# Gate projections drained by ScalarE and multiplied by the norm later, query transposes moved behind the value products

## The chip, the core and the metric

The kernel runs on one core of one Trainium2 chip. The core's engines run side by side, each through its own list of instructions in order: TensorE (PE, with its weight loads as PEld) multiplies matrices into PSUM, VectorE (DVE) and ScalarE (ACT) work elementwise on PSUM and SBUF, GpSimd (POOL) on SBUF, and SyncE (SP) issues DMAs. Semaphores order work across engines. The metric is device time in microseconds (us) of one execution.

## The reference

One layer of a hybrid decoder, batch 1, 512 tokens, width 1024, in fp32:

```python
h = rmsnorm(x, g_mix)
x_rnn, g_rnn, q, k, v, gate_a, gate_b = split(h @ w_in)
y_a = (rg_lru(causal_conv(x_rnn)) * gelu(g_rnn)) @ w_rnn_proj
y_b = window_attention(rope(rmsnorm(q)), rope(rmsnorm(k)), v, sinks) @ w_attn_proj
merged = sigmoid(gate_a) * y_a + sigmoid(gate_b) * y_b
x = x + merged @ w_out
x = x + square(relu(rmsnorm(x, g_mlp) @ w_up)) @ w_down
x = x + (p @ w_ple_proj) * sigmoid(rmsnorm(x, g_ple) @ w_ple_gate)
```

There are 16 query heads and 4 key-value heads of width 64; the window is 128 tokens, worked in four blocks of 128.

## The kernel before

All large products are made of three fp32r matmuls each, on weights and activations that are split into a high and a low part. A unit of weights (128 x 1024) comes from HBM, ACT writes its high part `wh` (line 118) and DVE the low part `wl` (line 119); `wload` keeps about three units ahead. The order on PE, ACT, SP and POOL is the order of the code (`manual_schedule`). DVE is not in that list: its order is set by the framework's scheduler, which may put an instruction far from where it stands in the code.

The change lies in the attention loop, eight turns `u` (four blocks of tokens for each half of the heads). The norm of x is not applied to the activations; `rb` holds the reciprocal norm of every token, and results are multiplied by it. Each turn has two groups of four heads, `g` = 0 and 1, and two gate projections, `p0` and `p1`, of 24 matmuls each, which fill PE between the steps of the softmax. On PE a turn is:

scores `S` of group 0; projection `p0`; transposes `ppt` of the previous turn's group 1 probabilities; scores of group 1; the previous turn's products with the values, `po`; the first half of `p1`; the transposes `pqt` of the next turn's queries; the second half of `p1`; transposes `ppt` of this turn's group 0.

For each group the softmax runs over the engines: ACT (or DVE, in the first block) copies scores out of PSUM into `sm`, DVE masks, takes the maximum and four small steps on `st` (lines 457 to 468), ACT takes the exponentials with their sums (474, 477), DVE adds and inverts (482, 483), POOL scales the probabilities in four instructions (486), PE transposes them and DVE masks the result into `pt`, twice (505), which `po` reads. `sm` has two buffers, the score bank `S` one.

The queries are turned by `q_rope` on DVE (lines 405 to 408: `ra`, twice `rb`, and `ra` again), transposed on PE, and split into `qt` by ACT (423) and DVE (425). A gate projection is taken out of PSUM by DVE, which multiplies it by `rb` (596); its sigmoid comes later, in the recurrent branch (750) or ahead of the merge (798).

Of the kernel before, what the change touches and what calls it, by code (L numbers as in the profile page):

```python
# [9 lines left out]
F32 = mybir.dt.float32  # L10
F32R = mybir.dt.float32r
AF = mybir.ActivationFunctionType
ALU = mybir.AluOpType
# [57 lines left out]
def layer_kernel(ctx, tc, w_all, x_t, p_t, vecs, row, ctab, out_t):  # L71
    nc = tc.nc
# [19 lines left out]
    def ftile(name):  # L92
        return act.tile([P, S], F32, tag="f", name=name, bufs=F_BUFS)
# [11 lines left out]
    def wissue(parts=1):  # L105
        u = order.pop(0)
        ready[u] = wsplit(u, wp, W_BUFS, parts)
# [15 lines left out]
    def wload(u):  # L123

        while u not in ready or (order and len(ready) <= AHEAD):
            wissue()
        return ready.pop(u)
# [110 lines left out]
    def s_ps(name):  # L238
        return ps.tile([P, 4, 256], F32, tag="S", name=name, bufs=1)

    def s_banks(name):
        wide = s_ps(name).rearrange("p a b -> p (a b)")
        return [wide[:, 0:S], wide[:, S : 2 * S]]
# [151 lines left out]
    def q_rope(u):  # L395
        n = u % NB
        src = q_raw.pop(u).rearrange("p (h d) -> p h d", d=HD)
        a = ftile(f"ra_{u}").rearrange("p (h d) -> p h d", d=HD)
        b = ftile(f"rb_{u}").rearrange("p (h d) -> p h d", d=HD)
        tt = nc.vector.tensor_tensor  # L400

        def tb(t, lo, hi):
            return t[:, n, lo:hi].unsqueeze(1).broadcast_to([P, 8, hi - lo])

        tt(out=a, in0=src, in1=tb(ccq, 0, HD), op=ALU.mult)
        tt(out=b[:, :, 0:32], in0=src[:, :, 32:64], in1=tb(ssq, 0, 32), op=ALU.mult)
        tt(out=b[:, :, 32:64], in0=src[:, :, 0:32], in1=tb(ssq, 32, 64), op=ALU.mult)
        tt(out=a, in0=a, in1=b, op=ALU.add)
        q_rot[u] = a

    def q_transpose(u, pt=None):


        a = q_rot.pop(u)
        pt = tr_ps(f"pqt{u}") if pt is None else pt
        for i in range(4):
            nc.tensor.transpose(pt[:, i * P : (i + 1) * P],
                                a[:, 2 * i : 2 * i + 2, :].rearrange("p a d -> p (a d)"), ident)
        qt = [att.tile([P, 4, P], F32R, tag="qt", name=f"qt{u}{j}", bufs=4) for j in range(2)]
        rows = [slice(0, HD), slice(HD, P)]  # L420
        src = [pt[own].rearrange("p (i t) -> p i t", t=P) for own in rows]
        for j, own in enumerate(rows):
            nc.scalar.activation(qt[j][own], src[j], AF.Copy)
        for j, own in enumerate(rows):
            nc.vector.tensor_tensor(out=qt[j][rows[1 - j]], in0=src[j],
                                    in1=qt[j][own].bitcast(F32), op=ALU.subtract)
        q_t[u] = qt

    def window(u):
        n = u % NB  # L430
        return max(n - 1, 0), (2 if n else 1)
# [78 lines left out]
    def pv(u):  # L510
        po = mm_ps(f"po{u}")
        b0, nb = window(u)
        for kb in range(nb):
            for g in range(2):
                kv = 2 * (u // NB) + g
                nc.tensor.matmul(po[g * HD : (g + 1) * HD, :],
                                 vt[:, b0 + kb, kv * HD : (kv + 1) * HD],
                                 p_t_.pop((u, g, kb)), start=kb == 0, stop=kb == nb - 1)
        return po.rearrange("p (i t) -> p i t", t=P)

    def o_split(u, po):
        t = slice(u % NB * P, (u % NB + 1) * P)
        oj = o[u // NB]
        nc.scalar.activation(oj[:, :, 0, t], po, AF.Copy)
        nc.vector.tensor_tensor(out=oj[:, :, 1, t], in0=po, in1=oj[:, :, 0, t].bitcast(F32),
                                op=ALU.subtract)
# [49 lines left out]
    def q_first():  # L576
# [5 lines left out]
    qkv_group(2, q_banks, [  # L582
        lambda: (k_transpose(norm["rot"]), q_first()),
        k_double,
        lambda: q_transpose(0, s_banks("pqt0")[0]),
    ])
    rb = norm["x"]
    q_evac(1, q_banks)
# [4 lines left out]

    def gate_evac(pg, name):
        gt = ftile(name)
        nc.vector.tensor_tensor(out=gt, in0=pg, in1=rb, op=ALU.mult)
        gates.append(gt)

    fills = [U_GB + m for m in range(KC)] + [U_GA + m for m in range(KC)]

    for u in range(8):
        w0 = wload(fills[len(gates)])
        p0 = mm_ps(f"pgate_{u}_0")
        s0 = scores(u, 0)
        softmax_max(u, 0, s0)
        proj(p0, w0, xg)
        if u:
            p_transpose(u - 1, 1)
            p_evac(u - 1, 1)
        softmax_exp(u, 0)  # L610
        if u < 7:
            q_rope(u + 1)
        softmax_norm(u, 0)
        if u < 6:
            q_scale(u + 2)
        gate_evac(p0, f"gate_{u}_0")
        s1 = scores(u, 1)
        if u:
            o_split(u - 1, pv(u - 1))
        softmax_max(u, 1, s1)  # L620
        w1 = ready.pop(fills[len(gates)])
        p1 = mm_ps(f"pgate_{u}_1")
        proj(p1, w1, xg, range(0, CUT))
        if u < 7:
            q_transpose(u + 1)
        wissue()
        softmax_exp(u, 1)
        softmax_norm(u, 1)
        proj(p1, w1, xg, range(CUT, KC))
        gate_evac(p1, f"gate_{u}_1")  # L630
        p_transpose(u, 0)
        p_evac(u, 0)
# [91 lines left out]
    for m in range(KC + LAG):  # L724
        if m < KC:
            w = wload(U_X + m)
            px = mm_ps(f"px{m}")
            proj(px, w, xg, range(0, 5))
            if m == 0:
                p_transpose(7, 1)  # L730
                p_evac(7, 1)
            proj(px, w, xg, range(5, 8))
            if m == 0:
                po = pv(7)
                o_split(7, po)
                att_scope.close()
                rnn = rnn_scope.enter_context(tc.tile_pool(name="rnn", bufs=1))
                gw += wsplit(U_GATE, rnn, 1)
        if py_last:
            att_evac(*py_last)  # L740
        for f in later.pop(0):
            f()
        later.append([])
        if m < KC:
            x_scale(m, px)
        units = gate_units((m - 3, m - 2)) if m in (3, 5, 7) else []
        if m < KC:
            x_conv(m)
        for gt in gb[m : m + 1]:
            nc.scalar.activation(gt, gt, AF.Sigmoid)  # L750
        if m >= LAG:
            w = wload(U_ATT + m - LAG)
            py_last = m - LAG, mm_ps(f"pyb{m - LAG}")
            for g in units:
                gate_post(*g)
            proj(py_last[1], w, o)
        if len(batch) == 2:
            take_pair()
# [6 lines left out]
    for m in range(KC):  # L765
# [4 lines left out]
        pg = mm_ps(f"pgl{m}")  # L770
# [24 lines left out]

    mg = rtiles("mg")
    for gt in ga:
        nc.scalar.activation(gt, gt, AF.Sigmoid)
    first = [(wload(U_RNN + m), mm_ps(f"pya{m}")) for m in range(2)]
    for w, py in first:  # L800
# [16 lines left out]
    for m in range(KC):  # L817
# [3 lines left out]
        po = mm_ps(f"pout{m}")  # L821
# [65 lines left out]
    for m in range(KC):  # L887
        w = wload(U_PG + m)
        pg = mm_ps(f"ppg{m}")
# [90 lines left out]
```

## Time and profile before

| | us |
|---|---|
| median of 3 runs | 838.13 (837.47, 838.13 and one of 2166.76) |
| the profiled execution | 837.6 |
| its span, first to last instruction | 835.5 |
| PE busy | 829.4 |
| DVE busy | 522.1 |
| ACT busy | 365.0 |
| POOL busy | 101.4 |
| granted TensorE clock, mean | 0.999 |

Busy time is the sum of an engine's recorded instructions. PE's records overlap each other, since matmuls are pipelined, and a matmul that starts late behind a wait can be recorded as part of a longer busy stretch; so PE's share says that little else ends the kernel, and the spacing of its starts says how long each thing takes. The profiled execution is 0.5 us under the median and 2.1 us longer than its span.

### The profile page before, as it was taken

The numbers are of one execution on the slowest core, as the hardware profiler recorded it, in microseconds if no ns is written. First come the engines' busy times: TensorE is split into PE (matmuls) and PEld (weight loads), VectorE is DVE, ScalarE is ACT, GpSimd is POOL, SyncE is SP. The second block draws the span as 40 slices with busy tenths as digits, with TensorE's granted clock in tenths as the row PEclk, the third lists the DMA queues.
The fourth block names the chain that finished last, engine by engine and source line by source line (L and its number), as shares of the span: only waits on it lengthen the run. The fifth ranks groups of instructions, "written<-read, shape, count | busy, mean of one in ns | idle before, by whom it ended". The sixth has DMA issues, their size and how long they took to land.

```text
span 835.5 us, 9915 instructions
## 1 busy us (share of the span) xinstructions
PE 829.4 (99%) x3780; PEld 678.9 (81%) x3780; DVE 522.1 (62%) x768; ACT 365.0 (44%) x581; POOL 101.4 (12%) x123
## 2 busy tenths in 40 slices
PE   9999999999999999999999999999999999999997
PEld 7888877877888888888888888888888888888886
DVE  4687798886766878486567533653355435655563
ACT  7434665663578895633343221231222212333430
POOL 2922432421011110000210000000000000012100
PEclk9999999999999999999999999999999999999999
DMA  7344122122232232235333322223223232233141
GB/s 251 126 115 138 51 80 72 51 77 76 76 100 76 76 102 100 76 127 186 131 103 109 104 98 102 89 89 119 86 97 100 101 102 76 100 102 101 51 163 39
DMA packets 25744, 84.00 MB, mean 101 GB/s; under 512 B 3040, under 2 KB 3424, under 8 KB 25696
## 3 DMA queue, kind: packets, MB, share of 16 engines
q1 hardware_dynamic: 25552, 83.32, 30.0%
q8 instruction: 30, 0.49, 0.2%
q14 instruction: 18, 0.15, 0.1%
q10 hardware_dynamic: 144, 0.05, 0.0%
HBM read 80.20 MB, written 2.10 MB: 99 GB/s over the span
## 4 chain that ended last, share of the span: by engine, by line
PE 99%; DMA 0%; DVE 0%; ACT 0%; issue 0%
PE pu L145 7%; PE pd L145 7%; PE pd L147 7%; PE pu L147 7%; PE pd L146 7%; PE pu L146 7%; PE pq L258 5%; PE pgate L145 4%; PE pgate L147 4%; PE pgate L146 4%; PE pkv L258 3%; PE pyb L145 2%; PE S L441 2%; PE px L145 2%; PE pgl L145 2%; PE pyb L146 2%
## 5 line engine op out<-in xcount | busy, mean ns | idle before, releaser
L119 DVE TENSOR_TENSOR wl<-wr,wh 128x1024 fp32r<-128x1024 f32 (+1 forms) x144 | 180.6, 1257 | 56.1 <-ACT wh L118 56.1
L118 ACT ACTIVATE wh<-wr 128x1024 fp32r<-128x1024 f32 (+1 forms) x144 | 149.7, 1045 | 130.5 <-PE pd L146 98.5
L146 PE MATMUL pu<-x1g,wh 128*128 128x512 f32 x256 | 99.6, 389 | 0.0
L145 PE MATMUL pu<-x1g,wh 128*128 128x512 f32 x256 | 99.6, 389 | 0.0
L147 PE MATMUL pu<-x1g,wl 128*128 128x512 f32 x256 | 99.6, 389 | 0.0
L145 PE MATMUL pd<-u,wh 128*128 128x512 f32 x256 | 99.6, 389 | 0.0
L146 PE MATMUL pd<-u,wh 128*128 128x512 f32 x256 | 99.6, 389 | 0.0
L147 PE MATMUL pd<-u,wl 128*128 128x512 f32 x256 | 99.6, 389 | 0.0
L131 ACT ACTIVATE u<-up 128x512 fp32r<-128x512 f32 x32 | 20.2, 633 | 124.4 <-DVE up L847 124.4
L213 POOL TENSOR_TENSOR sq<-sq,sq_x 128x512 f32<-128x512 f32 x14 | 18.2, 1298 | 453.5 <-ACT sq_x L211 453.5
L856 DVE TENSOR_TENSOR xr<-pd,xr 128x512 f32<-128x512 f32 x32 | 22.1, 692 | 81.5 <-PE pd L147 81.5
L147 PEld LDWEIGHTS pu<-x1g,wl 128*128 128x128 f32 x256 | 48.0, 188 | 10.1
L147 PEld LDWEIGHTS pd<-u,wl 128*128 128x128 f32 x256 | 48.0, 188 | 10.0
L146 PEld LDWEIGHTS pd<-u,wh 128*128 128x128 f32 x256 | 48.0, 188 | 10.0
L146 PEld LDWEIGHTS pu<-x1g,wh 128*128 128x128 f32 x256 | 48.1, 188 | 10.0
L145 PEld LDWEIGHTS pd<-u,wh 128*128 128x128 f32 x256 | 48.0, 188 | 9.9
L145 PEld LDWEIGHTS pu<-x1g,wh 128*128 128x128 f32 x256 | 48.0, 188 | 9.9
L145 PE MATMUL pgate<-xg,wh 128*128 128x512 f32 x128 | 51.4, 402 | 0.0
L147 PE MATMUL pgate<-xg,wl 128*128 128x512 f32 x128 | 50.2, 392 | 0.0
L146 PE MATMUL pgate<-xg,wh 128*128 128x512 f32 x128 | 50.0, 391 | 0.0
L846 DVE TENSOR_TENSOR up<-pu,rb_x 128x512 f32<-128x512 f32 x32 | 22.0, 691 | 40.2 <-PE pu L147 40.1
L474 ACT ACTIVATE sm<-sm,st,sc 128x128 f32<-128x128 f32 x64 | 30.8, 483 | 23.6 <-DVE st L468 21.6
(225 smaller groups left out, 1620.1 us busy)
## 6 DMA issues: line engine op xcount, KB each, us to landing
wr<-in_w_all SPq DMA_DIRECT2D x142, 512.0 KB, 3.3
x<-in_x_t SPq DMA_DIRECT2D x8, 256.0 KB, 5.6
xr<-in_x_t SPq DMA_DIRECT2D x8, 256.0 KB, 3.6
out<-pgt SPq DMA_DIRECT2D x7, 256.0 KB, 2.1
kt<-kt SPq DMA_DIRECT2D x8, 128.0 KB, 2.2
wr<-in_w_all SPq DMA_DIRECT2D x2, 256.0 KB, 3.6
pk<-in_p_t SPq DMA_DIRECT2D x2, 256.0 KB, 3.8
tab<-in_ctab SPq DMA_DIRECT2D x1, 384.0 KB, 6.8
```

The costliest lines, as they stand in the source:

```text
L118: nc.scalar.activation(wh[:, c], raw[:, c], AF.Copy)
L119: nc.vector.tensor_tensor(out=wl[:, c], in0=raw[:, c], in1=wh[:, c].bitcast(F32), op=ALU.subtract)
L131: nc.scalar.activation(r[:, 0, :], src, AF.Copy)
L145: nc.tensor.matmul(out, ah, bh, start=start, stop=False)
L146: nc.tensor.matmul(out, ah, bl, start=False, stop=False)
L147: nc.tensor.matmul(out, al, bh, start=False, stop=stop)
L213: nc.gpsimd.tensor_tensor(out=acc, in0=acc, in1=t, op=ALU.add)
L258: nc.tensor.matmul(banks[n], a[:, part, n * P : (n + 1) * P], w[:, c], start=k == 0 and i == 0, stop=k == KC - 1 and i == 2)
L441: nc.tensor.matmul(pss[:, i, :], q_t[u][i % 2][:, 2 * g + i // 2, :], kt[part][:, kv, b0 * P : b0 * P + 256], start=part == 0, stop=part == 1)
L474: nc.scalar.activation(sm[:, i, :], sm[:, i, :], AF.Exp, bias=st[:, 1, i : i + 1], scale=q_sc[u][:, 4 * g + i : 4 * g + i + 1], accum_out= ...
L846: nc.vector.tensor_tensor(out=y, in0=pu, in1=r1, op=ALU.mult)
L856: nc.vector.tensor_tensor(out=x1[m], in0=pd, in1=x1[m], op=ALU.add)
```

## The change

Three edits. The gate projection leaves PSUM through ACT, as a plain copy; the product with `rb` is written in the code ahead of each gate's sigmoid. The transposes of the next queries move on PE from the middle of `p1` to the place behind `po`, in turns 1 to 6; their evacuation to `qt` stays where it was on ACT. So that the queries are turned in time, `q_rope(u + 1)` moves in the code from behind the exponentials of group 0 to the start of turn `u`.

```diff
     def q_transpose(u, pt=None):
...
-        for j, own in enumerate(rows):
-            nc.scalar.activation(qt[j][own], src[j], AF.Copy)
-        for j, own in enumerate(rows):
-            nc.vector.tensor_tensor(out=qt[j][rows[1 - j]], in0=src[j],
-                                    in1=qt[j][own].bitcast(F32), op=ALU.subtract)
         q_t[u] = qt
+        def evac():
+            for j, own in enumerate(rows):
+                nc.scalar.activation(qt[j][own], src[j], AF.Copy)
+            for j, own in enumerate(rows):
+                nc.vector.tensor_tensor(out=qt[j][rows[1 - j]], in0=src[j],
+                                        in1=qt[j][own].bitcast(F32), op=ALU.subtract)
+        return evac
...
     def gate_evac(pg, name):
         gt = ftile(name)
-        nc.vector.tensor_tensor(out=gt, in0=pg, in1=rb, op=ALU.mult)
+        nc.scalar.activation(gt, pg, AF.Copy)
...
     for u in range(8):
+        if 0 < u < 7:
+            q_rope(u + 1)
...
         softmax_exp(u, 0)
-        if u < 7:
-            q_rope(u + 1)
+        if u == 0:
+            q_rope(1)
         softmax_norm(u, 0)
...
         if u:
-            o_split(u - 1, pv(u - 1))
+            po = pv(u - 1)
+            qt_evac = q_transpose(u + 1) if u < 7 else None
+            o_split(u - 1, po)
...
         if u < 7:
-            q_transpose(u + 1)
+            (qt_evac if u else q_transpose(1))()
...
         for gt in gb[m : m + 1]:
+            nc.vector.tensor_tensor(out=gt, in0=gt, in1=rb, op=ALU.mult)
             nc.scalar.activation(gt, gt, AF.Sigmoid)
...
     for gt in ga:
+        nc.vector.tensor_tensor(out=gt, in0=gt, in1=rb, op=ALU.mult)
         nc.scalar.activation(gt, gt, AF.Sigmoid)
```

In the changed kernel the lines behind the first edit are three higher (408 stays, 425 becomes 428, 482 becomes 485), and the products with `rb` are lines 757 and 806.

First place: DVE around the exponentials of group 0 in turn 2. `st_1047` (before) and `st_1053` (after) hold the small columns of that group; L468, or L471 now, is the last step ahead of the exponentials, L482, or L485 now, the first that needs them. Before:

```order
L468 TENSOR_TENSOR st_1047<-rowb,st_1047 128x4
L505 TENSOR_TENSOR pt_1082<-ppt_1077,tab 128x512
L505 TENSOR_TENSOR pt_1084<-ppt_1077,tab 128x512
L405 TENSOR_TENSOR ra_1091<-q_518,cc_q 128x512
L406 TENSOR_TENSOR rb_1092<-q_518,ss_q 128x8x32
L407 TENSOR_TENSOR rb_1092<-q_518,ss_q 128x8x32
L482 TENSOR_TENSOR st_1047<-st_1047 128x4
L388 TENSOR_REDUCE sc_1105<-asq_1103 128x8
L408 TENSOR_TENSOR ra_1091<-ra_1091,rb_1092 128x512
L483 RECIPROCAL st_1047<-st_1047 128x4
L390 TENSOR_SCALAR sc_1105<-sc_1105,e_180 128x8
L596 TENSOR_TENSOR gate_0_1109<-pgate_0_1034,rb_x 128x512
```

The same place after:

```order
L471 TENSOR_TENSOR st_1053<-rowb,st_1053 128x4
L485 TENSOR_TENSOR st_1053<-st_1053 128x4
L486 RECIPROCAL st_1053<-st_1053 128x4
L388 TENSOR_REDUCE sc_1105<-asq_1103 128x8
L757 TENSOR_TENSOR gate_0_1109<-gate_0_1109,rb_x 128x512
L390 TENSOR_SCALAR sc_1105<-sc_1105,e_180 128x8
L528 TENSOR_TENSOR o_706<-po_1120,o_706 128x4x128
```

The two `pt` and the rope no longer stand between the step ahead of the exponentials and the step behind them; the gate's product stays in the loop.

Second place: DVE from the inversion of turn 1, group 1 (`st_958` before, `st_965` after), which releases POOL's scaling, to the small steps of turn 2, group 0. Before:

```order
L505 TENSOR_TENSOR pt_1026<-ppt_1019,tab 128x512
L482 TENSOR_TENSOR st_958<-st_958 128x4
L483 RECIPROCAL st_958<-st_958 128x4
L119 TENSOR_TENSOR wl_1030<-wr_1028,wh_1029 128x1024
L457 COPY_PREDICATED sm_1044<-tab,S_1035 128x512
L464 TENSOR_REDUCE st_1047<-sm_1044 128x4
```

After:

```order
L486 RECIPROCAL st_965<-st_965 128x4
L405 TENSOR_TENSOR ra_1028<-q_518,cc_q 128x512
L406 TENSOR_TENSOR rb_1029<-q_518,ss_q 128x8x32
L407 TENSOR_TENSOR rb_1029<-q_518,ss_q 128x8x32
L119 TENSOR_TENSOR wl_1036<-wr_1034,wh_1035 128x1024
L408 TENSOR_TENSOR ra_1028<-ra_1028,rb_1029 128x512
L460 COPY_PREDICATED sm_1050<-tab,S_1041 128x512
L508 TENSOR_TENSOR pt_1088<-ppt_1083,tab 128x512
L467 TENSOR_REDUCE st_1053<-sm_1050 128x4
L508 TENSOR_TENSOR pt_1090<-ppt_1083,tab 128x512
L468 TENSOR_TENSOR st_1053<-st_1053,sc_775 128x4
L757 TENSOR_TENSOR gate_1_1017<-gate_1_1017,rb_x 128x512
```

The rope, both `pt` of turn 1's group 1 and the product of its second gate now stand ahead of L471 of turn 2; `pt_1088` reads `ppt_1083`, PE's transposes of what POOL scales behind L486.

Third place: ACT from the exponentials of turn 1's group 1 to those of turn 2's group 0, after the change.

```order
L480 ACTIVATE st_965<-st_965 128x4
L599 ACTIVATE gate_1_1017<-pgate_1_971 128x512
L118 ACTIVATE wh_1035<-wr_1034 128x1024
L459 ACTIVATE sm_1050<-S_1041 128x512
L477 ACTIVATE sm_1050,st_1053<-sm_1050,st_1053,sc_775 128x128 x4
```

Only the gate's copy, L599, is new there; the rest stood in that order before.

## Rows read from the trace of the kernel before

**Rows 1.** The page's part 4: the chain that ended last, by engine.
```profile
PE 99%; DMA 0%; DVE 0%; ACT 0%; issue 0%
```

**Rows 2.** Windows by turn: us; busy PE, PEld, DVE, ACT, POOL (count); clock; DMA.
```profile
94.66:110.25 15.59, 15.59 (x82) 12.28 (x81) 12.68 (x30) 9.50 (x27) 5.53 (x9) 1.00 0.17 53
110.25:125.83 15.58, 15.58 (x78) 12.05 (x78) 14.70 (x33) 9.60 (x27) 5.25 (x9) 1.00 0.20 70
...
159.36:174.92 15.56, 15.56 (x83) 12.42 (x82) 13.47 (x32) 9.50 (x28) 5.47 (x9) 1.00 0.18 56
...
190.13:203.78 13.65, 13.65 (x70) 10.33 (x69) 9.71 (x23) 7.22 (x22) 1.41 (x4) 1.00 0.19 64
```

**Rows 3.** Timeline of PE, turn 2 and turn 6: start, length, operation.
```profile
108.95 0.81 PE L494 MATMUL ppt<-ident,sm 128*128 128x128 f32 x4
109.51 1.19 PE L441 MATMUL S<-kt,qt 128*128 128x256 f32 x8
110.63 2.17 PE L516 MATMUL po<-pt,kv 128*64 128x512 f32 x8
...
115.59 0.60 PE L417 MATMUL pqt<-ident,ra 128*128 128x128 f32 x4
...
174.99 2.49 PE L516 MATMUL po<-pt,kv 128*64 128x512 f32 x8
```

**Rows 4.** Timeline of DVE, turn 2.
```profile
110.14 1.28 DVE L505 TENSOR_TENSOR pt<-ppt,tab 128x512 f32<-128x512 f32 x2
111.33 0.68 DVE L405 TENSOR_TENSOR ra<-q,cc_q 128x512 f32<-128x512 f32 x1
111.93 0.42 DVE L406 TENSOR_TENSOR rb<-q,ss_q 128x256 f32<-128x256 f32 x1
112.27 0.42 DVE L407 TENSOR_TENSOR rb<-q,ss_q 128x256 f32<-128x256 f32 x1
112.60 0.16 DVE L482 TENSOR_TENSOR st<-st 128x4 f32<-128x4 f32 x1
...
115.51 0.73 DVE L457 COPY_PREDICATED sm<-tab,S 128x512 f32<-128x512 int32 x1
116.28 0.69 DVE L464 TENSOR_REDUCE st<-sm 128x4 f32<-128x512 f32 x1
...
122.44 0.17 DVE L483 RECIPROCAL st<-st 128x4 f32<-128x4 f32 x1
122.53 1.23 DVE L119 TENSOR_TENSOR wl<-wr,wh 128x1024 fp32r<-128x1024 f32 x1
```

**Rows 5.** Timeline of ACT, turn 2.
```profile
110.25 0.49 ACT L474 ACTIVATE sm<-sm,st,sc 128x128 f32<-128x128 f32 x1 [2.70 <-DVE st L468]
...
112.17 0.19 ACT L477 ACTIVATE st<-st 128x4 f32<-128x4 f32 x1
112.27 0.61 ACT L386 ACTIVATE asq<-q 128x512 f32<-128x512 f32 x1
...
113.33 0.59 ACT L456 ACTIVATE sm<-S 128x512 f32<-128x512 f32 x1
116.29 1.21 ACT L423 ACTIVATE qt<-pqt 64x512 fp32r<-64x512 f32 x2 [2.36 <-PE pqt L417]
```

**Rows 6.** Timeline of POOL: the four scalings, end of turn 1, turn 2 twice.
```profile
106.91 2.46 POOL L486 TENSOR_SCALAR sm<-sm,st 128x128 f32<-128x128 f32 x4 [5.57 <-ACT wh L118]
114.48 1.41 POOL L486 TENSOR_SCALAR sm<-sm,st 128x128 f32<-128x128 f32 x4 [5.11 <-DVE sc L390]
...
122.81 2.23 POOL L486 TENSOR_SCALAR sm<-sm,st 128x128 f32<-128x128 f32 x4 [5.30 <-DVE st L483]
```

**Rows 7.** Timeline of POOL ahead of the loop: the first two products of `kv`.
```profile
41.02 3.47 POOL L326 TENSOR_SCALAR kv<-kv,rtok 128x256 f32<-128x256 f32 x2
```

**Rows 8.** Timeline of DVE beside them; all inputs lie in SBUF.
```profile
42.33 1.30 DVE L341 TENSOR_TENSOR krot<-kn,cc_k 128x1024 f32<-128x1024 f32 x1
43.55 0.68 DVE L196 TENSOR_TENSOR nt_x<-rb_x 128x512 f32<-128x512 f32 x1
```

More of the change, by code (lines that the diff above doesn't have):

```diff
@@ L584, in layer_kernel @@
         k_double,
-        lambda: q_transpose(0, s_banks("pqt0")[0]),
+        lambda: q_transpose(0, s_banks("pqt0")[0])(),
     ])
```

## Prediction

> **What bounds the kernel now.** I read the page's chain of waits first: PE ends it with 99% of the span [rows 1]. So a change elsewhere can gain only what PE loses in gaps, and can lose any amount if it makes PE wait. The edits all lie in the attention loop, so the next view is the busy time by window, one window for each turn, from the start of ACT's exponentials for the first group of heads to the same point a turn later [rows 2]. The reader is to see three things there: a turn lasts 15.6 us, the granted clock is 1.00, and DVE is busy for 14.70 us of 15.58. PE sets the pace, but DVE has under 1 us to spare in a turn.
>
> Then the timelines of turn 2. PE shows where it is nearly late already [rows 3]: the transposes of turn 1's second group took 0.81 us, where a neighbour of the same four takes 0.60, and in turn 6 the value products took 2.49 us against 2.17 in turn 2. These are waits inside busy time, 0.2 to 0.5 us each. On DVE I look at what stands in the time of the exponentials [rows 4, 5]. They last from 110.25 to 112.36, or 2.11 us, and the step that needs them, L482, comes at 112.60. In between DVE does two `pt` and three of the four rope operations. This is the cover on which the turn rests.
>
> **The gate projections.** Removed: 16 products on DVE that read PSUM. Added: 16 copies on ACT, for which I take ACT's copy of a score bank of the same size, 0.59 us [rows 5], so 0.6 us twice a turn on an engine that is busy for 9.60 us of 15.58 [rows 2]. Cost on the path: nothing while ACT has that room; in front of the small copies and `wh` it delays them by 0.5 us, which DVE, being later, hides. The products with the norm don't leave the loop: the scheduler puts L757 and L806 back among the attention work, all 16 of them. Reading SBUF alone, each is like L405, 0.68 us [rows 4]; before it was a product of the same width that read PSUM. I take the difference as nothing, so DVE's work in a turn stays at 14.7 us.
>
> **The transposes.** They stay four transposes a turn, 0.60 us [rows 3]; moved, they could share a switch of PE's with the value products or not. I take 0, with a bound of 0.1 us either way for each of six turns. ACT waited 2.36 us for them in turn 2 [rows 5]; that wait goes. It was not on the path, since what follows on DVE waited only briefly. What is late next is DVE itself.
>
> **The rope, and DVE's new order.** This is where the time goes. Between L471 and L485 nothing is left, so DVE now stands still for all of the exponentials. And the rope, with a weight split in its midst, now stands between the inversion of the previous turn's second group and the mask of this turn's first. I follow one turn from the start of the group 0 exponentials, as 0.0, with steps from rows. On DVE an operation that needs nothing new starts 0.08 us before its forerunner's recorded end (L406 after L405), one that needs the forerunner 0.04 us behind it (L464 after L457) [rows 4]. So a wide one takes 0.60 or 0.72, a 256-wide one 0.34, a weight split 1.14, a small one 0.08 or 0.20.
>
> - 0.0 to 2.11: exponentials, DVE idle. L485 and L486 end at 2.5.
> - L388 waits for `asq` (0.61 us behind the exponentials, [rows 5]) and ends at 3.35; the gate's product, L390, the split of `o` and the mask L460 follow freely: 5.31.
> - `qt`, L467, `qt`, L468, a weight split, L469 and L470: 8.74. The `qt` meet no wait to speak of, since ACT reaches them at 5.3.
> - Exponentials of group 1: 8.84 to 10.95. DVE fills them with one `pt` (to 9.4) and waits 1.5 us. Then L485, the other `pt` and L486, which ends at 11.84 and releases POOL's scaling at 12.0.
> - L405, L406, L407, the weight split and L408: 11.76 to 14.86.
> - POOL's scaling takes 1.41 us alone, 2.46 or 2.23 when it meets a weight split [rows 6]. So it stands behind DVE operations that read two operands from SBUF, and all five here do. Whether it stands behind a row of them is in rows ahead of the loop: a product of `kv` asked at 42.5, behind `krot`, which ended at 43.63; it ended at 44.49 [rows 7], 0.26 us after the next DVE operation, `nt_x`, had ended at 44.23 [rows 8]. I therefore let POOL start at 14.86: 0.2 for the first of four and 0.35 for each of the others, 16.1. PE's last transpose follows at 16.4.
> - L460 stands ahead of this on DVE and is done; both `pt` wait for that transpose. With L467, L468 and the gate's product between them, L470 ends at 19.3, and the next exponentials start at **19.4**.
>
> A rule bears on this. The Trainium skill, SBUF — State Buffer, section Who interferes with whom, says that such an instruction and GpSimd's exclude each other, that the second to issue waits until the first has finished, and that issue order decides. The row of `nt_x` shows DVE going first although POOL had asked earlier; by the rule POOL would slip in between two of the five, its scaling would end at about 15.5 and the five some 1.1 us later. The turn would come to about 19.6 and the whole to 1 us more than by the row; I take the row.
>
> A full turn thus takes 19.4 us against 15.6. PE's own work of a turn is in it: after its last transpose at 16.4 scores, value products (to 19.4, the second half waits for the second `pt`), queries, 48 gate matmuls, two more groups; it reaches the next such transposes at about 13, and waits 3 us.
>
> **The sum over turns.** Turn 0 has slack: its scaling ends before PE wants it, so turn 1's exponentials start at 94.7 as before. Turns 1 and 2 are full: turn 2's start at 114.1 (before 110.25), turn 3's at 133.5. Turn 3 holds the first block of the second half in its midst, whose mask DVE takes earlier; its last transposes come 17.0 us on, at 150.5. In turn 4 the probabilities leave PSUM through ACT, the rope is off the path, and PE is again the pace: turn 5's exponentials at 166.7, against 159.36 [rows 2], +7.3. Turn 5 is full: 186.1 for turn 6, against 174.92, +11.2. Turn 6 has no `asq` and no rope behind it: 203.3 for turn 7, against 190.13, +13.2. PE's slack at the end of turn 7 gives some back: the last probabilities are transposed at 215.4, against 203.78, **+11.6**. Behind that nothing waits that didn't before. To this I add about 0.15 us for each of six turns in which the gate's product at 3.3 meets POOL's scaling of group 0 (from 2.7 on), 0.9. So 12.5 us, and 837.6 + 12.5 = 850.1, as device time of the profiled execution, which is 0.5 under the median of the runs shown. I say **850**.
>
> Bounds. Above: if DVE's operations never overlapped, some 12 free ones in a turn would cost 0.08 more each, 1 us a turn, 5 us over five turns: 855. Below: if the five operations did not hold POOL, its scaling would end at 13.5, the `pt` would wait for nothing and the turn would be 18.4, 1 us less in each of five turns: 845; without the 0.9, and with the hidden waits [rows 3] and the switch given back, 842.
>
> **Rivals.**
> 1. *Not slower.* The transposes of the queries come 2.8 us earlier, ACT loses its 2.36 us wait, and all that follows on ACT and DVE runs early enough to pay for the rope. Then PE gets its hidden waits back, 0.2 and twice 0.2 to 0.5 us [rows 3]: 836.5 to 838. It decides at 13.2 in the turn above: if the scaling of group 1 ends before that, PE never waits. Against it: the wait was ACT's, and DVE's list alone, with 2.11 and 1.5 us of idling that had cover before, adds up to more than PE's turn.
> 2. *POOL is not held*, as bounded above: 842 to 845. For it: each of [rows 6] is held by one operation only. Against it: [rows 7, 8].
> 3. *The clock falls.* PE would stand idle for 3 us in each of four turns. All windows show 1.00 [rows 2], so no row here prices it. If it fell behind each such wait, matmuls would come at half their pace for a while; 3 us of them would cost 3 us a turn, of which DVE's longer turn hides a part, so 5 to 12 us in all: 855 to 862. The Trainium skill, TensorE: Matmul & The Clock Gate, section HAM oscillation — how this bites in real kernels, says that long idle gaps send TensorE back to the lower of its levels, 1.2 GHz; no run here shows it.
> 4. *The change does not do what it says* is partly so already: the norm's products are not deferred.
>
> **How the numbers follow.** The forecast, 845 to 855, gets 0.73; POOL not held 0.09; not slower 0.10; the clock 0.08. The range of 842 to 857 holds the forecast and POOL not held, and the lower part of the clock; it leaves out the first rival and the rest of the clock, 0.16. A difference of 2%, 16.8 us, is about what a measurement of this kernel can tell from no change. Slower by more than that, over 854.9, needs the upper end of the forecast or the clock: 0.16. Faster by 2% would need 17 us of gaps that PE does not have: 0.01. Within 2%: 0.83.
>
> **What would show it.** In the profile after: turns 1, 2 and 5 of 19 to 20 us from exponentials to exponentials; DVE idle behind ACT's exponentials ahead of L485; POOL's scaling of group 1 stretched to 3 or 4 us; PE idle about 3 us ahead of the `ppt` of group 1, released by POOL; the rest of the kernel unchanged to within 0.5 us. Wrong would be: turns of 15.6 us; or long turns with a short scaling, in which case DVE's list alone is the cause; or a granted clock below 1.00.

## The result, and the profile after

The changed kernel takes 851.86 us (median of 4 runs, 851.03 to 852.37) against 838.06: a ratio of 1.0165, 95% interval 1.0153 to 1.0177. The forecast was 850.0, with a range from 842 to 857. The profiled span is 849.8 us, 14.3 more than before, and all of it arises in the attention loop: its last `ppt` ends at 218.17 instead of 203.78, the first matmul of the up projection `pu` comes at 441.61 instead of 427.27.

The page's chain of waits that ended last, by engine, which was 99% PE before [rows 1]:

```profile
PE 87%; DVE 6%; ACT 4%; POOL 2%; issue 1%; DMA 0%; SPq 0%; POOLq 0%; ACTq 0%
```

The same windows as in [rows 2], from the exponentials of group 0 to those of the next turn, for turns 1, 2, 4 and 5 after the change:

```profile
94.88:114.42 19.54, 18.24 (x91) 13.07 (x89) 14.96 (x34) 10.36 (x28) 6.85 (x9) 1.00 0.18 63
114.42:133.87 19.45, 17.33 (x85) 12.84 (x84) 15.02 (x33) 10.36 (x29) 7.01 (x9) 1.00 0.17 55
147.40:169.41 22.01, 20.20 (x97) 14.19 (x97) 16.92 (x36) 11.09 (x31) 10.27 (x13) 0.92 0.21 71
169.41:188.83 19.42, 18.30 (x91) 13.12 (x90) 15.02 (x33) 10.35 (x30) 7.02 (x9) 1.00 0.17 57
```

In turn 2 DVE's busy time is nearly what it was, 15.02 us against 14.70. The turn is longer because DVE stands still for 4.4 us of it instead of 0.9. Turn 4 alone shows a clock under 1.00.

DVE in turn 2 of the changed kernel; the number in brackets is the idle time ahead, and who ended it (compare [rows 4]):

```profile
114.24 0.15 DVE L471 TENSOR_TENSOR st<-rowb,st 128x4 f32<-128x4 f32 x1
116.58 0.16 DVE L485 TENSOR_TENSOR st<-st 128x4 f32<-128x4 f32 x1 [2.18 <-ACT st L480]
...
123.76 0.69 DVE L508 TENSOR_TENSOR pt<-ppt,tab 128x512 f32<-128x512 f32 x1
125.92 0.16 DVE L485 TENSOR_TENSOR st<-st 128x4 f32<-128x4 f32 x1 [1.46 <-ACT st L480]
126.00 0.68 DVE L508 TENSOR_TENSOR pt<-ppt,tab 128x512 f32<-128x512 f32 x1
126.60 0.17 DVE L486 RECIPROCAL st<-st 128x4 f32<-128x4 f32 x1
126.68 0.66 DVE L405 TENSOR_TENSOR ra<-q,cc_q 128x512 f32<-128x512 f32 x1
127.26 0.42 DVE L406 TENSOR_TENSOR rb<-q,ss_q 128x256 f32<-128x256 f32 x1
127.60 0.51 DVE L407 TENSOR_TENSOR rb<-q,ss_q 128x256 f32<-128x256 f32 x1
128.03 1.21 DVE L119 TENSOR_TENSOR wl<-wr,wh 128x1024 fp32r<-128x1024 f32 x1
129.16 0.77 DVE L408 TENSOR_TENSOR ra<-ra,rb 128x512 f32<-128x512 f32 x1
129.86 0.72 DVE L460 COPY_PREDICATED sm<-tab,S 128x512 f32<-128x512 int32 x1
130.94 0.69 DVE L508 TENSOR_TENSOR pt<-ppt,tab 128x512 f32<-128x512 f32 x1 [0.36 <-PE ppt L497]
```

Both exponentials leave DVE idle, 2.18 and 1.46 us. POOL's scaling behind L486, and PE's transposes of it:

```profile
126.96 3.56 POOL L489 TENSOR_SCALAR sm<-sm,st 128x128 f32<-128x128 f32 x4 [6.37 <-DVE st L486]
```
```profile
128.26 0.27 PE L497 MATMUL ppt<-ident,sm 128*128 128x128 f32 x1
129.45 0.33 PE L497 MATMUL ppt<-ident,sm 128*128 128x128 f32 x1 [0.92 <-POOL sm L489]
130.23 0.68 PE L497 MATMUL ppt<-ident,sm 128*128 128x128 f32 x2 [0.45 <-POOL sm L489]
```

The scaling takes 3.56 us where the longest shown before took 2.46 [rows 6], and PE gets its four transposes in three portions over 2.6 us instead of 0.8 [rows 3]. PE waits at one more place of this turn: 0.73 us, until 122.20, for the second half of `qt` (L428).

### The profile page after: what moved, and what is told of

Read it like the earlier page. It is cut to its first block, busy times and chain, and to the rows that moved or that the text cites. A ratio compares the mean times of both kernels' runs of the same rounds, so it can differ in the third digit from the quotient of the medians.

```text
span 849.8 us, 9934 instructions
## 1 busy us (share of the span) xinstructions
PE 835.1 (98%) x3780; PEld 679.5 (80%) x3780; DVE 523.4 (62%) x768; ACT 372.2 (44%) x597; POOL 112.6 (13%) x123
## 4 chain that ended last, share of the span: by engine, by line
PE 87%; DVE 6%; ACT 4%; POOL 2%; issue 1%; DMA 0%; SPq 0%; POOLq 0%; ACTq 0%
PE pu L146 7%; PE pu L145 7%; PE pd L145 7%; PE pd L146 7%; PE pd L147 7%; PE pu L147 7%; PE pq L258 5%; PE pkv L258 3%; ACT sm L477 3%; PE pyb L145 2%; PE pgl L145 2%; PE ppg L145 2%; PE ppg L147 2%; PE pgl L146 2%; PE pyb L146 2%; PE pgl L147 2%
## 5 line engine op out<-in xcount | busy, mean ns | idle before, releaser
L213 POOL TENSOR_TENSOR sq<-sq,sq_x 128x512 f32<-128x512 f32 x14 | 18.2, 1297 | 453.7 <-ACT sq_x L211 453.7
L489 POOL TENSOR_SCALAR sm<-sm,st 128x128 f32<-128x128 f32 x60 | 39.3, 672 | 94.0 <-DVE st L486 45.8
```

The lines of the kernel that those rows point to most:

```text
L213: nc.gpsimd.tensor_tensor(out=acc, in0=acc, in1=t, op=ALU.add)
L489: eng.tensor_scalar(out=sm[:, i, :], in0=sm[:, i, :], scalar1=den[:, i : i + 1], scalar2=1.0, op0=ALU.mult, op1=ALU.mult)
```

## The experiments

Theory A, which stood behind the forecast: the order that DVE's list takes sets the length of a turn. The rivals named in the expectations are that one edit alone is the cause or costs by itself (the rope's place, ACT's copies, the transposes' place), that POOL's hold is the whole cause, and the clock. The table gives each run's median, its distance to the kernel before on the same chip, its ratio, and for turn 2 (exponentials to exponentials) the length, DVE's busy time and the difference, DVE's idling.

| run | us | change | ratio, 95% interval | turn 2 | DVE busy | idle |
|---|---|---|---|---|---|---|
| before | 838.06 | | | 15.58 | 14.70 | 0.88 |
| after | 851.86 | +13.8 | 1.0165 [1.0153, 1.0177] | 19.45 | 15.02 | 4.43 |
| gate edit alone | 849.36 | +11.3 | 1.0132 [1.0117, 1.0147] | 18.80 | 14.94 | 3.86 |
| rope and transposes | 839.78 | +1.7 | 1.0021 [1.0011, 1.0030] | 17.14 | 14.66 | 2.48 |
| transposes alone | 842.70 | +4.6 | 1.0053 [1.0038, 1.0068] | 16.01 | 14.69 | 1.32 |
| rope alone | 842.70 | +4.6 | 1.0054 [1.0039, 1.0069] | 17.98 | 14.59 | 3.39 |
| group 1 scaled by DVE | 850.65 | +12.9 | 1.0157 [1.0142, 1.0173] | 19.55 | 15.51 | 4.04 |
| PE's waits filled | 848.42 | +10.7 | 1.0130 [1.0116, 1.0143] | 18.96 | 14.91 | 4.05 |
| after, gates deferred | 847.43 | +9.7 | 1.0116 [1.0102, 1.0129] | 18.45 | 13.96 | 4.49 |
| that, rope put back | 842.34 | +4.6 | 1.0061 [1.0048, 1.0074] | 16.13 | 13.58 | 2.55 |
| after, rope pinned | 843.71 | +5.6 | 1.0067 [1.0051, 1.0082] | 18.28 | 14.82 | 3.46 |
| pinned and deferred | 841.76 | +3.7 | 1.0044 [1.0031, 1.0057] | 17.74 | 13.84 | 3.90 |
| before, gates deferred | 840.16 | +2.1 | 1.0023 [1.0012, 1.0033] | 17.47 | 14.46 | 3.01 |
| that, `pt` pinned | 840.44 | +2.3 | 1.0029 [1.0018, 1.0040] | 16.71 | 14.04 | 2.67 |

### Which edit

**Gate edit alone**, in the kernel before:

```diff
     def gate_evac(pg, name):
-        nc.vector.tensor_tensor(out=gt, in0=pg, in1=rb, op=ALU.mult)
+        nc.scalar.activation(gt, pg, AF.Copy)
...
         for gt in gb[m : m + 1]:
+            nc.vector.tensor_tensor(out=gt, in0=gt, in1=rb, op=ALU.mult)
...
     for gt in ga:
+        nc.vector.tensor_tensor(out=gt, in0=gt, in1=rb, op=ALU.mult)
```

> The kernel before with the gate edit alone: ACT copies the gate projection, DVE's products with the norm stand later in the code; rope and transposes as before. DVE's order changes all the same: both `pt` of the last group 1 and half of the rope now stand ahead of the last step before the exponentials of group 0 (L468), and a gate product stands between the inversion and the weight split. Theory A (DVE's new order sets the turn, whichever edit makes it): the exponentials of group 0 keep 1.0 us of cover instead of 2.1, POOL's scaling of group 1 is held by two DVE operations, a turn comes to about 18.3 us, the kernel to about 845. Theory B (the rope's place alone is the cause): 838, turns of 15.6. Theory C (the copies burden ACT): turns of up to 16.8, two copies of 0.6 more, with ACT as the one waited for; 844, DVE not idle behind the exponentials.

It cost 11.3 us, more than A said and far from B's nothing: the edit that the prediction had priced at nothing brings most of the loss. ACT does 0.8 us more in a turn, but DVE idles behind the exponentials, 1.40 us behind those of turn 1's group 1 and 1.13 behind those of turn 2's group 0, so C as it was stated falls too. Nor is it more work on DVE: its busy time in turn 2 is 14.94 us, 0.24 more than before, in a turn that is 3.2 us longer. DVE from turn 1's group 1 to turn 2's group 0 in this run, where L468 is the last step ahead of the exponentials, L483 the inversion and L457 the mask:

```profile
106.28 0.16 DVE L482 TENSOR_TENSOR st<-st 128x4 f32<-128x4 f32 x1 [1.40 <-ACT st L477]
...
106.96 0.17 DVE L483 RECIPROCAL st<-st 128x4 f32<-128x4 f32 x1
107.05 0.66 DVE L750 TENSOR_TENSOR gate<-gate,rb_x 128x512 f32<-128x512 f32 x1
...
109.02 0.72 DVE L457 COPY_PREDICATED sm<-tab,S 128x512 f32<-128x512 int32 x1
...
112.33 0.68 DVE L405 TENSOR_TENSOR ra<-q,cc_q 128x512 f32<-128x512 f32 x1
...
113.00 0.42 DVE L406 TENSOR_TENSOR rb<-q,ss_q 128x256 f32<-128x256 f32 x1
...
113.41 0.16 DVE L468 TENSOR_TENSOR st<-rowb,st 128x4 f32<-128x4 f32 x1
```

The rope stands in the same line of the code as before, but DVE's order has its first half ahead of L468, and the gate's product between the inversion and the mask.

**Rope and transposes** without the gate edit, **rope alone**, **transposes alone**:

```diff
# rope alone
     for u in range(8):
+        if 0 < u < 7:
+            q_rope(u + 1)
...
-        if u < 7:
-            q_rope(u + 1)
+        if u == 0:
+            q_rope(1)
# transposes alone (q_transpose is split in two as in the change)
...
-            o_split(u - 1, pv(u - 1))
+            po = pv(u - 1)
+            qt_evac = q_transpose(u + 1) if u < 7 else None
+            o_split(u - 1, po)
...
-            q_transpose(u + 1)
+            (qt_evac if u else q_transpose(1))()
```

> The changed kernel without the gate edit: DVE multiplies the gates out of PSUM as in the kernel before; rope at the start of the turn, transposes behind the value products. Theory A: the rope stands between the inversion of group 1 and the mask, with only half of it under the exponentials of group 1, and the gate's product is the only cover of the exponentials of group 0: a turn of about 17.1 us, the kernel about 844. Theory B (the rope's place is the whole cause, the gate edit free): 850 to 852, turns of 19.4. Theory D (moving the rope costs nothing by itself, all is the gate edit): 838.

> The kernel before with the rope alone moved to the start of the turn; transposes and gates as before. Theory A: as in the changed kernel the rope with a weight split in it stands between inversion and mask, but the gate's product covers 0.7 us of the exponentials of group 0 and two rope operations lie under those of group 1: a turn of about 17.1, the kernel about 844. Theory B (the rope's place is the whole cause): 850 to 852. Theory D (all is the gate edit): 838.

> The kernel before with the transposes of the queries alone moved behind the value products; rope and gates as before. DVE's order stays but for one gate product, which now stands ahead of the rope's last operation. Theory A: PE waits for that operation, at first by about 1.2 us, until DVE runs that much ahead; 839.5, turns of 15.6 to 16, exponentials of group 0 still covered. Theory E (the transposes' place itself costs): 0.6 us or more in each of six turns for good, 842 or more.

Rope and transposes together gave the turn that A worked out, 17.07 and 17.14 us in turns 1 and 2, but only 1.7 us in the end: turns 1, 2, 3 and 5 lost 6.7 us, and turns 4 and 6, with 14.5 and 14.3 us where the kernel before has 17.3 and 15.2, gave 3.8 of them back, turn 7 another 1. With the gates taken by DVE from PSUM, the exponentials of group 1 are covered; DVE there, with no wait ahead of L485:

```profile
104.04 1.28 DVE L508 TENSOR_TENSOR pt<-ppt,tab 128x512 f32<-128x512 f32 x2
105.23 0.68 DVE L405 TENSOR_TENSOR ra<-q,cc_q 128x512 f32<-128x512 f32 x1
105.83 0.42 DVE L406 TENSOR_TENSOR rb<-q,ss_q 128x256 f32<-128x256 f32 x1
106.24 0.16 DVE L485 TENSOR_TENSOR st<-st 128x4 f32<-128x4 f32 x1
```

The rope alone cost 4.6, near A's 6 and not B's 12. The transposes alone cost 4.6 too, where A had said 1.5: PE waits for the rope not once but in four turns (2, 3, 4 and 6), by 1.1 to 1.2 us each and 4.7 together. Turns 2 and 3:

```profile
114.02 0.66 PE L417 MATMUL pqt<-ident,ra 128*128 128x128 f32 x4 [1.21 <-DVE ra L408]
...
131.35 0.66 PE L417 MATMUL pqt<-ident,ra 128*128 128x128 f32 x4 [1.11 <-DVE ra L408]
```

So E's size was right and its cause was not: the place costs nothing once the rope is early (both together are 2.9 us faster than either). The gate edit's 11.3 and the pair's 1.7 make 13.0 of the 13.8, though nothing says that they must add up.

### DVE's order, POOL's hold, or the work

**Group 1 scaled by DVE**, in the changed kernel:

```diff
-            eng = nc.vector if (u, g) == (7, 1) else nc.gpsimd
+            eng = nc.vector if g == 1 else nc.gpsimd
```

> The changed kernel with the four scalings of every group 1 done by DVE instead of POOL (they stand behind the rope's first operation). POOL is not used there, so nothing of it can be held; DVE has about 1 us more in a turn. Theory A (DVE's list sets the turn, the hold of POOL adds about 1 us to it): a turn of about 18.6 us instead of 19.4, the kernel 846 to 848. Theory F (POOL held behind DVE is the whole cause): turns of 15.6 to 16.6, 838 to 842. Theory G (the hold costs nothing): 1 us more in a turn, 855 or more.

The turn stayed at 19.48 and 19.55 us, which ends theory F: with no scaling on POOL there to hold, DVE's list is just as long. A's size was missed by 1 us a turn. The four scalings cost DVE 0.87 us, so the run does not price the hold by itself; what the hold did to DVE in the changed kernel is its wait for the `ppt`, 0.63 us in turn 1 and 0.36 in turn 2. PE's transposes are free at once, and PE waits for the next scores instead, whose bank DVE's mask empties:

```profile
109.61 0.60 PE L497 MATMUL ppt<-ident,sm 128*128 128x128 f32 x4
112.51 2.08 PE L444 MATMUL S<-kt,qt 128*128 128x256 f32 x8 [2.29 <-DVE sm L460]
```

**After, gates deferred.** The products also multiply by a column of ones that ACT writes behind the loop:

```diff
     gb, ga = gates[:KC], gates[KC:]
+    late = const.tile([P, 1], F32, name="late")
+    nc.scalar.activation(late, rb[:, 0:1], AF.Identity, scale=0.0, bias=1.0)
...
-            nc.vector.tensor_tensor(out=gt, in0=gt, in1=rb, op=ALU.mult)
+            nc.vector.scalar_tensor_tensor(out=gt, in0=gt, scalar=late, in1=rb,
+                                           op0=ALU.mult, op1=ALU.mult)
```

> The changed kernel with the gates' products truly deferred: they also multiply by a column of ones that ACT writes behind the loop, so that DVE cannot take them earlier. In the loop DVE has two products of 0.6 us less in a turn; rope and transposes as in the changed kernel. Theory A: the idling behind the exponentials and the rope between inversion and mask stay, the turn is shorter by the two products, 18.2 us instead of 19.4, the kernel 844 to 846. Theory D (the hoisted gate products are the whole cause): turns of 15.6, 838.

D falls: two products less in a turn brought 1.0 us a turn and 4.1 us in all, and a turn is still 18.5. A's 18.2 was close; its 844 to 846 was missed by 1.4 us. DVE has 0.7 us less to do than in the kernel before and idles 4.5 us. Less work does not help a list whose waits stay.

**After, rope pinned.** The work stays but for one tiny operation, and the rope's place in DVE's order changes: the sum L485 of group 1 needs a zero that is made from the rope's third operation. For that the rope moves in the code half a turn ahead, to the exponentials of group 1 of the turn before.

```diff
     def q_rope(u, zero=None):
...
+        if zero is not None:
+            nc.vector.tensor_scalar(out=zero, in0=b[:, 0, 63:64], scalar1=0.0, scalar2=None,
+                                    op0=ALU.mult)
...
+            nc.vector.scalar_tensor_tensor(out=den, in0=den, scalar=zero, in1=st[:, 3],
+                                           op0=ALU.add, op1=ALU.add)
...
-        if 0 < u < 7:
-            q_rope(u + 1)
...
         softmax_exp(u, 1)
-        softmax_norm(u, 1)
+        zero = None
+        if u < 6:
+            zero = att.tile([P, 1], F32, tag="zero", name=f"zero{u}", bufs=2)
+            q_rope(u + 2, zero)
+        softmax_norm(u, 1, zero)
```

> The changed kernel with all three edits, and DVE's order pinned at one place: the sum behind the exponentials of group 1 (L485) also adds a zero that is made from the rope's third operation, so that the rope cannot stand behind the inversion any more. The rope then lies ahead of and under the exponentials of group 1; only a weight split stands between the inversion and the mask, so that POOL's scaling is held by one operation. One tiny operation more in each turn. Theory A (DVE's order sets the turn): a turn of 16.6 to 17.2 us instead of 19.4, scaling of 2.5 instead of 3.4 us, the kernel 839 to 843. Theory C (the edits cost by themselves, by the copies on ACT or by work on DVE): turns of 18.5 or more, 848 or more.

All three edits are in, and 8.2 of the 13.8 us are gone. This is the run that shows the order as the cause: the copies stay, and DVE's work in turn 2 is 14.82 us against 15.02. Up to 1.7 of the 8.2 us are the fall of the clock that the changed kernel shows in turn 4 and this run does not (see the clock, below); at least 6.5 are the order's. A's 839 to 843 was missed by 0.7. The turns (18.0 and 18.3) are longer than A had worked out: group 0's exponentials stay bare, with up to 3.6 us of waiting, and ACT's `wh`, behind the gate's copy, lets the weight split wait 0.55 to 0.61. POOL's scaling at the end of turn 2, beside 3.56 above:

```profile
126.48 2.38 POOL L496 TENSOR_SCALAR sm<-sm,st 128x128 f32<-128x128 f32 x4 [6.37 <-DVE st L493]
```

**Pinned and deferred**, both edits together:

> As the run with the rope pinned, and the gates' products truly deferred as well. Theory A: a turn of 16 to 16.5 us, with 2.1 us of idling behind the exponentials of group 0 as all that is left of the loss; 837 to 840. If the idling behind the exponentials of group 0 by itself sets the turn, it stays at 17 or more and the kernel at 842 or more.

841.76, between the two branches, with a turn of 17.7: the idling behind group 0's exponentials (2 us and more) lengthens the turn, and only part of it reaches PE.

### The clock

**PE's waits filled**, in the changed kernel:

```diff
+N_FILL = 10
...
         pt = tr_ps(f"ppt{u}{g}")
+        if g == 1 and u in (1, 2, 3, 5):
+            for _ in range(N_FILL):
+                nc.tensor.matmul(pt, xg[0][:, 0, 0, 0:P], xg[0][:, 0, 0], start=True, stop=True)
```

> The changed kernel with ten matmuls of 512 columns, 2.1 us, added on PE ahead of the transposes of group 1 in the four turns in which PE waits there for 2.4 us or more; their result is overwritten. They fill the wait and nothing else. Theory H (the one fall of the granted clock, 3.4 us at 0.50 behind the longest of these waits, costs about 1.8 us): the clock stays at 1.00 and the kernel comes to 850.0. Rival (the fall lies in time that PE would wait anyway): the clock stays at 1.00 and the kernel at 851.9. If the fall has another cause, the clock falls as before and the time is 851.9 or more.

The changed kernel's clock fell once, behind turn 4's wait for POOL (`ppt` from 147.94 to 150.96). Windows of 1 us there (the clock is the third number from the right), then the scores and value products, and the next transposes, those of turn 4's group 0:

```profile
152.00:153.00 1.00, 1.00 (x4) 0.33 (x4) 1.00 (x5) 0.00 (x0) 0.00 (x0) 0.50 0.00 0
...
154.00:155.00 1.00, 1.00 (x4) 0.00 (x0) 0.00 (x0) 0.00 (x0) 1.00 (x3) 0.50 0.00 0
155.00:156.00 1.00, 1.00 (x7) 0.60 (x6) 0.00 (x0) 0.46 (x1) 1.00 (x1) 0.83 0.00 0
```
```profile
150.72 1.18 PE L444 MATMUL S<-kt,qt 128*128 128x256 f32 x8
151.84 3.63 PE L519 MATMUL po<-pt,kv 128*64 128x512 f32 x8
...
161.40 0.60 PE L497 MATMUL ppt<-ident,sm 128*128 128x128 f32 x4
```

The same place with the waits filled, where the clock stays at 1.00:

```profile
149.73 1.18 PE L445 MATMUL S<-kt,qt 128*128 128x256 f32 x8
150.84 1.94 PE L523 MATMUL po<-pt,kv 128*64 128x512 f32 x8
...
158.69 0.60 PE L501 MATMUL ppt<-ident,sm 128*128 128x128 f32 x4
```

From the start of the scores to that of the transposes it is 10.68 us against 8.96, so the fall cost 1.72. Turn 5's exponentials start 18.69 and 16.97 us behind the same scores, again 1.72 apart. The run as a whole gained 3.1, not 1.8: DVE also took a gate product in its wait for `ppt`, and turns 1, 2 and 5 are 0.5 to 0.7 shorter. The total is therefore no test of the clock; the two stretches of PE are.

Whole executions show a fall's price too. Those of the changed kernel had a mean granted clock of 0.997 three times (851.85 to 852.37 us) and 0.999 once (851.03); those of the run "after, gates deferred", whose trace has such a fall as well, 0.998 twice (848.13 and 848.17) and 0.999 and 1.000 (846.73 and 846.24). The ones with the lower clock are 0.8 to 1.9 us longer, and the fall seems not to come in every execution.

### Gates on ACT without the rest

**That, rope put back** (copies, deferred products, transposes behind `po`, rope at its old place):

> The changed kernel with the gates' products truly deferred, as in the run before, and the rope back behind the exponentials of group 0; ACT's copies and the transposes behind the value products stay. DVE's order around the exponentials is that of the kernel before, with 1.2 us less work in a turn. Theory A: both `pt` and three rope operations cover the exponentials again, PE sets the pace and its small hidden waits shrink: 836.5 to 838, turns of 15.4 to 15.6. Rivals: the transposes wait for the rope in every turn: 840 to 844; or the 16 products taken later delay the recurrent branch: 838 to 842, with turns of 15.6 and a longer rest.

A's value failed, the first rival came: DVE does 1.1 us less in turn 2 and group 0's exponentials are covered, and PE waits for the rope (0.66 us in turn 2, 1.14 in turn 3, and in turns 4 and 6) as in the run with the transposes alone; both are at +4.6.

**Before, gates deferred** (rope and transposes as before):

> The kernel before with the gates copied by ACT and their products truly deferred behind the loop; rope and transposes as before. Against the run with the gate edit alone, only the 16 products leave the loop, and with them DVE's order goes nearly back: the rope stands behind the last step ahead of the exponentials of group 0 (L468), both `pt` between the small steps ahead of it. Theory A (DVE's order, not the copies): the four rope operations cover 1.9 of the 2.1 us of exponentials, a turn of 15.6 to 16, 836.5 to 839. Theory C (ACT's copies cost by themselves): most of the 11.3 us of the gate edit stays, 845 or more.

Only 2.1 of the gate edit's 11.3 us are left when the products cannot be taken early. That settles against C for 9.2 us, not for the rest. A's 836.5 to 839 was missed as well, and its turn of 15.6 to 16 came out as 17.5. The run takes the two products a turn off DVE too, so it does not part order from work; the gate edit alone does that, with 14.94 us of work in a turn of 18.80.

**That, `pt` pinned**: a one made from L468's result is a factor of both `pt`, so that they stand under the exponentials as before.

```diff
+                    nc.vector.scalar_tensor_tensor(out=out, in0=i0, scalar=one, in1=i1,
+                                                   op0=ALU.mult, op1=ALU.mult)
...
+            one = att.tile([P, 1], F32, tag="one", name=f"one{u}", bufs=2)
+            nc.vector.tensor_scalar(out=one, in0=probs[u, 0][1][:, 3, 0:1], scalar1=0.0, scalar2=1.0,
+                                    op0=ALU.mult, op1=ALU.add)
-            p_evac(u - 1, 1)
+            p_evac(u - 1, 1, one)
```

> The kernel before with the gates copied by ACT and truly deferred, as in the run that came to 840.2, and both `pt` of the last group 1 pinned behind the last step ahead of the exponentials of group 0 (L468): they also multiply by a one that is made from that step's result. DVE's order around the exponentials is then that of the kernel before: both `pt` and three rope operations under the exponentials. Rope and transposes stand where they stood. Theory A: the copies on ACT cost nothing, the 2.1 us of the run before came from the `pt` among the small steps; turns of 15.4 to 15.7 and 836.5 to 838.5, so at best a little under the kernel before, since DVE has 1.2 us less to do in a turn and PE's small hidden waits shrink. Theory C (ACT's copies, or the products taken later, cost by themselves): 840 as in that run.

A missed: 840.44, no better than the run before it, though around group 0's exponentials DVE's order is again that of the kernel before. What differs is read on ACT and DVE in turn 2:

```profile
122.59 0.60 ACT L600 ACTIVATE gate<-pgate 128x512 f32<-128x512 f32 x1
123.08 1.05 ACT L118 ACTIVATE wh<-wr 128x1024 fp32r<-128x1024 f32 x1
```
```profile
118.54 0.68 DVE L425 TENSOR_TENSOR qt<-pqt,qt 64x512 fp32r<-64x512 f32 x1 [1.14 <-ACT qt L423]
...
124.17 1.27 DVE L119 TENSOR_TENSOR wl<-wr,wh 128x1024 fp32r<-128x1024 f32 x1 [0.72 <-ACT wh L118]
125.36 0.74 DVE L457 COPY_PREDICATED sm<-tab,S 128x512 f32<-128x512 int32 x1
```

The copy stands 0.5 us ahead of `wh`, the split waits for it, and the mask stands behind the split; before, the split started 0.09 after the inversion's start [rows 4], here 0.89 after it (L483 starts at 123.28). DVE's wait for `qt` is longer as well, 1.14 us where it was 0.36. In this turn the exponentials of group 1 come 0.46 us later behind those of group 0 than before, and the next turn's 0.67 us later behind them. How much of the 2.3 us in all is the wait for `wh` and how much the pin itself (the one, and 0.1 more for two `pt`) was not taken apart, so whether ACT's copies cost something by themselves stays open. No kernel here beats the one before.

## Why the forecast was right, and where its steps were not

**The turn.** 19.4 was forecast, 19.54, 19.45 and 19.42 measured in turns 1, 2 and 5. The idling was read rightly (2.11 and 1.5, measured 2.18 and 1.46), as was the end of POOL's scaling, 16.1 behind the exponentials (130.52 against 114.42). That the end came out so well is luck, since two errors cancelled on the way: group 1's exponentials came at 9.34, not 8.84, mostly because the steps between the `qt` took longer; and the scaling needed 3.56 us from its release, not 4.1. POOL was not kept behind all five DVE operations, as the forecast had it: two of its four scalings were done before the fifth operation, L408, ended at 129.93, since PE's second transpose starts at 129.45; the row ahead of the loop that it took for its pattern [rows 7, 8] did not carry over. That POOL gets in between fits what the Trainium skill says in SBUF — State Buffer, Who interferes with whom, that issue order decides; but the delay that I had worked out from it, 1.1 us for the five, measured 0.15 (3.25 from L405 to L408's end, forecast 3.10). PE lost 2.0 us at these transposes, not 3 (2.65 from the first one's start to the last one's end, 0.60 alone): it reached them 13.8 us behind the exponentials, not 13, after the wait of 0.73 us for `qt` that the forecast did not have.

**The gate projections: "nothing".** This step failed as an account of cause. The copies left DVE's work alike, as written, but alone the edit costs 11.3 us, with another order on DVE; with the products held behind the loop 2.1 are left. That the scheduler could build that order because a product which reads SBUF no longer has to free a PSUM bank is a reading of the code that no run tests. The prediction's sum came out since it followed the order of all three edits together. That DVE hides the copy in front of `wh` held in the changed kernel, where the rope stands ahead of the split; with the rope or the `pt` pinned the split waits 0.55 to 0.72 us in turns 1 and 2.

**The rope: "this is where the time goes".** Half true. The rope between inversion and mask is what made the changed kernel slow (pinning it away gave 8.2 us back, up to 1.7 of them the clock's), but it costs 4.6 alone and 1.7 with the transposes. It becomes dear together with the gate edit: then nothing on DVE covers group 0's exponentials, and one `pt` alone those of group 1.

**The transposes: 0.** No run takes this edit out of the changed kernel, so its price there is not shown; ACT's wait for them is gone, as written. Without the gate edit it was not 0: beside the early rope the moved transposes gain 2.9 us, more than the bound of 0.1 a turn, and with the rope late they cost 4.6.

**The sum over turns.** Turn 2's exponentials came at 114.42 (forecast 114.1), turn 3's at 133.87 (133.5), the transposes behind them ended at 150.96 (150.5). Then the forecast fell behind: turn 5's came at 169.41, not 166.7. Of the 2.7, 1.72 is the clock and 0.46 was there already; the other 0.5 was not followed up. The loop ended 14.4 late instead of 12.5, and nearly all of that difference is the clock's 1.72. The 0.15 us a turn for the gate product's meeting with POOL's scaling shows in turn 2 as L390 taking 0.34 us, where it took 0.20 before.

**The rivals.** Not slower: excluded. POOL not held: it was held, but this rival's 1 us a turn was too much, since DVE waits only 0.63 and 0.36 us for the held transposes in turns 1 and 2. The clock fell, once and not behind each wait, and cost 1.7 instead of 5 to 12; it came on top of the forecast, not in its place. That the products are not deferred: true, and it is worth 4.1 us. The prediction also took 2% for about what a measurement of this kernel can tell from no change; the four times of the changed kernel lie within 1.4 us, 0.2%, so a difference of a few us shows.

## What to carry to other kernels

When one engine's order is left to a scheduler, an edit that only frees an instruction from its place (here from a PSUM bank) can cost far more than the work that it moves: read the new order for what covers each wait and what stands between a release and the next chain. Count an engine's waits, not its busy time: with 0.7 us less work a turn than the kernel before, and 4.5 us of waits, a turn was still 2.9 us longer. And an edit that moves a consumer forward is priced with its producer: the transposes alone and the rope alone lost 4.6 us each, together 1.7.

## What the hardware showed

A row of DVE operations with two SBUF operands did not shut POOL out: its four scalings, which take 1.41 us undisturbed [rows 6], took 3.56, and two of them were done before the last of the five operations ended, while two of the five grew, from 0.42 to 0.51 and from 0.68 to 0.77 us. TensorE's granted clock fell to 1.2 GHz for about 3.4 us behind the longest stretch in which PE's four transposes waited for POOL in the changed kernel (3.0 us from the first one's start to the last one's end), but not behind three others of 2.4 to 2.7 us. In the run "after, gates deferred" it fell behind such a stretch of 2.9 us and not behind one of 2.5; with the gate edit alone, where they reach 2.4 us, not once. The length of the wait does not settle it: in the run with DVE's scaling, where PE waits for the scores, it fell twice (0.92 and 0.94 mean in turns 1 and 2), at waits of 2.29 and 1.78 us, and not at a third one of 2.29.
